# SSM products as two diagonal blocks, with the tables kept without their zero blocks

## The chip, the cores and the metric

The kernel runs on one core of one Trainium2 chip. The metric is the time of one execution on the device, in microseconds; a lower time is better. The times before are the median, the lowest and the highest of three runs. One further execution was profiled, and all rows of a profile in this document come from such an execution. The engines are named as in the profile: PE (TensorE matmuls), PEld (its weight loads), DVE (VectorE), ACT (ScalarE), POOL (GpSimd) and SP (SyncE, which here only issues DMAs). A name with a q (SPq, ACTq) is the engine's instruction queue, where DMA issues show.

## The reference, cut to what matters

One layer of a decoder: a SwiGLU block, a mixer with a state-space part (SSM) and windowed attention side by side, and a second SwiGLU block, for 256 prompt positions and 8 sequences of 4 sample positions. The SSM part is the one that the change touches. It has 64 groups of 16 channels with 64 complex states each:

```python
def s5_mixer(u, h0, A_re, A_im, B_re, B_im, C_re, C_im, D, log_dt, w_glu):
    lam_bar = jnp.exp(lam * dt)
    B_bar = ((lam_bar - 1.0) / lam)[..., None] * Bc
    bu = jnp.einsum('blgc,gpc->blgp', u32.astype(jnp.complex64), B_bar)
    bu = bu.at[:, 0].add(lam_bar * h0)
    a = jnp.broadcast_to(lam_bar, bu.shape)
    _, h = lax.associative_scan(_ssm_combine, (a, bu), axis=1)
    y = jnp.einsum('blgp,gcp->blgc', h, Cc).real + D.astype(f32) * u32
    y = jax.nn.gelu(y)
    y = y * jax.nn.sigmoid(jnp.einsum('blgc,gcd->blgd', y, w_glu.astype(f32)))
    return y, h[:, -1]
```

No group's input ever meets another group's states, so a product over two groups at once has two diagonal blocks and zeros elsewhere.

## The kernel before

**Columns.** All 288 positions lie in the free dimension: 4 phases of 72 columns (T = 4, W1 = 72: 8 sample columns and 64 prompt chunks). The SSM works on chunks of four positions. The 64 groups form 8 tiles (j = 0 to 7) of 4 pairs (q), two groups (g) to a pair; 128 partitions hold either 2 groups x 64 states, or 4 phases x 2 groups x 16 channels = 128 inputs of a pair.

**Slots.** The work is laid out by the weights (class `Weights`). They come in pieces of up to 128 x 1024; each piece is a slot. `W.next()` opens slot i: ACT casts piece i+2 into `wh` (L89), DVE subtracts to get the rest `wl` (L90), SP issues the load of piece i+5 (L81), then the extra work queued for slot i is issued, and then PE runs the piece: 24 matmuls of 288 columns for 1024, 18 for 768 and 15 for 640 (L273 to L275). `raw` has 5 buffers, `wh` and `wl` have 3. Within an engine the order is that of the program.

The first SwiGLU block takes slots 0 to 303: gate/up pieces (1024) in 0-51, a down phase in 52-83 (768, "12-wide"), gate/up to 131, down in 132-163 (12-wide), gate/up to 203, down in 204-235 (640, "10-wide"), gate/up to 271, and the last down phase in 272-303. The mix stage begins with slot 304.

**The tables (`precompute`).** From slot 24 on, one step per slot (`W.spread(24, precompute(qp))`, a step ends at a `yield`) computes each tile's SSM tables beside the first SwiGLU block. `common` has 31 steps, then `tile_tables(j)` 24 for each tile, counted from 0. Steps 14 and 15 of a tile turn the input tables (`bed`, L566) on PE and evict them (L568), step 16 makes the impulse response (L572), steps 17 to 20 copy it into place (L579 to L589), and step 22 writes the whole `stage` of the tile, six blocks of 128 x 512, to `mats[j]` in DRAM by one ACT DMA (L593). The blocks are: input table re and im (0, 1), impulse block (2), output table re and im (3, 4), rotation (5). In blocks 0 to 4 half of the entries are zeros, where one group of a pair would meet the other; `stage` and `bed` are cleared once (L446) and only the other halves are written.

**The mix stage.** For each tile j, with s = 304 + 2j + 5, extra work is queued for slots: `ssm_u_store` (ACT DMA of the projected input to `ud`, s), `ssm_load_a` (SP, blocks 0 and 1, s), `ssm_u_load` (SP, four DMAs that bring `ud` back in the order of phases, s+2), `ssm_load_r` (SP, s+2), `ssm_state` (PE L733, from s+5 on, then DVE and POOL for the scan), `ssm_load_b` (SP, blocks 2 to 4, s+6), `ssm_out` (PE L773 to L775, s+9), `ssm_y_store` (ACT, four DMAs, s+10), `ssm_y_load` (SP, `yn` and `gl`, s+11), `ssm_glu` (s+13). Tiles follow each other two slots apart, so that one period of two slots holds a state product, an output product, four U loads and four y stores, each of another tile.

**DMA semaphores.** The program gives the DMAs of SP and ACT eight completion semaphores in turn; a DMA that takes a semaphore waits for the one that had it eight DMAs before, whichever queue that was on.

Of the kernel before, what the change touches and what calls it, by code (L numbers as in the profile page):

```python
# [17 lines left out]
P = 128  # L18
# [99 lines left out]
def tile_hymba_step(ctx, tc, io):  # L118
# [226 lines left out]
    mats = [dr.tile([P, 5 * 512 + 512], F32, name="mats%d" % j) for j in range(8)]  # L345
# [5 lines left out]
    def precompute(qp):  # L351
# [10 lines left out]
        cst = small("cst", (P, 16 + 2 + NCH + 5))  # L362
        are, aim, ldt, dco = (prm[:, 32 * i:min(32 * i + 32, 104)] for i in range(4))
        eye, mgi, nrow, n5 = cst[:, 0:16], cst[:, 16:18], cst[:, 18:18 + NCH], cst[:, 18 + NCH:]
# [7 lines left out]
        stage = small("stage", (P, 6, 4, P))  # L372
        bed = [small("bed%d" % i, (P, 4, 4, 2, 16)) for i in range(2)]
        rep = [small("rep%d" % i, (P, 4, 2, 16)) for i in range(2)]
        small("gap_p", (P, 24))
# [62 lines left out]
        def common():  # L438
# [6 lines left out]
            for t_ in [stage] + bed + rep:  # L445
                pool_e.memset(t_, 0.0)  # L446
# [72 lines left out]
        def halves(ap):  # L519

            return [ap[64 * g:64 * g + 64].rearrange("p q (j g d) -> p q j g d", j=4, g=2)[:, :, :, g, :]
                    for g in range(2)]

        def tile_tables(j):
# [35 lines left out]
            rot = stage[:, 5].rearrange("p q (s k) -> p q s k", s=2)  # L560
            yield from cos_sin(rot[:, :, 0, :], rot[:, :, 1, :], f, t)
            yield
            for i in range(2):
                ps = pa.tile([P, 512], F32, name="main")
                for q_ in range(4):
                    pe.transpose(ps[:, q_ * P:(q_ + 1) * P],  # L566
                                 bed[i][:, q_].rearrange("p j g c -> p (j g c)"), ident)
                act.copy(stage[:, i].rearrange("p q m -> p (q m)"), ps)  # L568
# [24 lines left out]
            act.dma_start(mats[j], stage.rearrange("p a q m -> p (a q m)"))  # L593
# [38 lines left out]
def mix(tc, nc, io, es, W, base, e):  # L632
# [71 lines left out]
    def ssm_u_load(j):  # L704
        U[j] = sm.tile([P, 4, W1], F32, name="U", bufs=4)
        src = ud[j].rearrange("(q c) (j t) -> j c q t", q=4, j=T)
        for jr in range(T):
            get(U[j][32 * jr:32 * jr + 32], src[jr])
# [14 lines left out]
    def ssm_load_b(j):  # L723
        MB[j] = sm.tile([P, 3, 4, P], F32, name="mb", bufs=2)
        get(MB[j].rearrange("p a q m -> p (a q m)"), e["mats"][j][:, 1024:2560])
# [545 lines left out]
```

## Time and profile before

| | |
|---|---|
| median of 3 runs (lowest, highest) | 1998.82 us (1998.45, 1999.53) |
| the profiled execution | 1999.87 us, of which its span is 1998.1 |
| granted TensorE clock | 1.00 throughout |
| issue of `U<-ud` (SP) | 32 DMAs of 36 KB |
| issue of `yd<-yg` (ACT) | 32 DMAs of 36 KB |
| issue of `mats<-stage` (ACT) | 8 DMAs of 1536 KB |

Engines by stage, from the profile's windows (the columns are the stretch in us, its length, busy time of PE, PEld, DVE, ACT and POOL with the number of instructions, the granted clock, the share of the DMA engines and GB/s):

```profile
205.00:720.00 515.00, 515.00 (x3915) 514.15 (x3915) 328.46 (x553) 224.27 (x361) 47.10 (x81) 1.00 0.58 189
...
865.00:1000.00 135.00, 132.52 (x1039) 130.59 (x1039) 105.79 (x210) 49.26 (x90) 32.44 (x71) 1.00 0.77 251
```

The first stretch holds the tables of the eight tiles, the second the SSM part of the mix stage. A row of the chain or of a timeline begins with its start and its length in us, both from the span's start; a bracket at its end is the idle time ahead of it and what ended that. "xN" is the number of records merged in a row.

### The profile page before, as it was taken

To read this page: it belongs to the slowest core of one execution; us is meant where nothing else is said; L and a number is where in the kernel's file an instruction comes from. 1 tells how busy PE (TensorE), PEld (TensorE's weight loads), DVE (VectorE), ACT (ScalarE), POOL (GpSimd) and SP (SyncE) were. 2 spreads that over 40 slices of the span, in tenths; PEclk is the share of its full clock that TensorE was granted. 3 is DMA by queue.
4 is the path that set the end of the run, shared out by engine and by line. 5 is a ranking of instruction groups with operands and counts; after the bars stand their busy time and mean duration, and the time that the engine had idled before them with its cause. 6 is when DMAs were issued, how large, how long until landed. Compare 5 with 4: busy or idle time off the path is not lost.

```text
span 1998.1 us, 37634 instructions
## 1 busy us (share of the span) xinstructions
PE 1980.5 (99%) x15256; PEld 1968.0 (98%) x15256; DVE 1219.0 (61%) x1874; ACT 852.0 (43%) x1334; POOL 296.0 (15%) x450
## 2 busy tenths in 40 slices
PE   8999999999999999999999999999999999999999
PEld 7999999999999999999989999999999999999999
DVE  5577666566666654677888874555555455555554
ACT  5443444443444443543476553333333333333333
POOL 3110011000100000211368640000000000000000
PEclk9999999999999999999999999999999999999999
DMA  7555655546555664678744445555555555555555
GB/s 237 188 169 152 198 168 201 193 151 209 198 180 155 215 201 142 216 248 265 247 132 132 154 159 169 169 155 172 181 169 162 160 186 169 157 157 193 169 154 158
DMA packets 122622, 359.04 MB, mean 180 GB/s; under 512 B 22448, under 2 KB 30256, under 8 KB 121264
## 3 DMA queue, kind: packets, MB, share of 16 engines
q1 hardware_dynamic: 114672, 340.81, 53.5%
q10 hardware_dynamic: 7776, 15.83, 2.3%
q8 instruction: 119, 1.95, 0.4%
q14 instruction: 55, 0.45, 0.1%
HBM read 338.40 MB, written 20.22 MB: 179 GB/s over the span
## 4 chain that ended last, share of the span: by engine, by line
PE 96%; DMA 1%; POOL 1%; DVE 0%; SPq 0%; ACT 0%; issue 0%; POOLq 0%; ACTq 0%; DVEq 0%
PE main L273 31%; PE main L275 31%; PE main L274 31%; POOL acc L191 1%; PE main L733 1%; DMA yd<-yg 0%; PE main L566 0%; PE main L572 0%; DMA x<-in_x 0%; PE main L988 0%; DMA raw<-in_w_gu 0%; PE main L775 0%; PE main L774 0%; PE main L956 0%; PE main L773 0%; PE main L975 0%
## 5 line engine op out<-in xcount | busy, mean ns | idle before, releaser
L90 DVE TENSOR_TENSOR wl<-raw,wh 128x1024 fp32r<-128x1024 f32 (+2 forms) x680 | 758.6, 1116 | 526.2 <-ACT wh L89 521.1
L273 PE MATMUL main<-xh,wh 128*128 128x288 f32 x3136 | 924.4, 295 | 6.7 <-ACT xh L181 6.4
L275 PE MATMUL main<-xh,wl 128*128 128x288 f32 x3136 | 919.0, 293 | 2.2 <-DVE wl L90 2.2
L274 PE MATMUL main<-xl,wh 128*128 128x288 f32 x3136 | 918.4, 293 | 0.6 <-DVE xl L182 0.6
L89 ACT CAST wh<-raw 128x1024 fp32r<-128x1024 f32 (+2 forms) x680 | 643.1, 947 | 600.2 <-PE main L274 385.4
L273 PEld LDWEIGHTS main<-xh,wh 128*128 128x128 f32 x3136 | 589.5, 188 | 8.0 <-ACT xh L181 6.4
L275 PEld LDWEIGHTS main<-xh,wl 128*128 128x128 f32 x3136 | 589.3, 188 | 3.0 <-DVE wl L90 2.9
L274 PEld LDWEIGHTS main<-xl,wh 128*128 128x128 f32 x3136 | 589.5, 188 | 1.4 <-DVE xl L182 1.0
L273 PE MATMUL main<-hh,wh 128*128 128x288 f32 x1664 | 489.8, 294 | 0.0
L274 PE MATMUL main<-hl,wh 128*128 128x288 f32 x1664 | 487.9, 293 | 0.3 <-DVE hl L684 0.3
L275 PE MATMUL main<-hh,wl 128*128 128x288 f32 x1664 | 487.8, 293 | 0.0
L274 PEld LDWEIGHTS main<-hl,wh 128*128 128x128 f32 x1664 | 312.6, 188 | 0.7 <-DVE hl L684 0.5
L273 PEld LDWEIGHTS main<-hh,wh 128*128 128x128 f32 x1664 | 312.5, 188 | 0.5 <-DVE t L1095 0.2
L275 PEld LDWEIGHTS main<-hh,wl 128*128 128x128 f32 x1664 | 312.5, 188 | 0.0
L300 POOL TENSOR_TENSOR s<-s,R 128x288 f32<-128x288 f32 x88 | 71.3, 810 | 1228.0 <-ACT s L299 1228.0
L299 ACT ACTIVATE s<-t 128x288 f32<-128x288 f32 x88 | 39.2, 445 | 233.5 <-DVE t L298 233.5
L309 ACT CAST hh<-h 128x288 fp32r<-128x288 f32 x88 | 38.2, 434 | 235.5 <-DVE h L308 235.5
L330 DVE SCALAR_TENSOR_TENSOR x<-main,x 128x288 f32<-128x288 f32 x128 | 58.4, 456 | 52.3 <-PE main L275 51.1
L308 DVE TENSOR_TENSOR h<-main,s 128x288 f32<-128x288 f32 x88 | 40.2, 457 | 70.3 <-PE main L275 69.9
L298 DVE TENSOR_TENSOR t<-main,R 128x288 f32<-128x288 f32 x88 | 40.2, 457 | 59.4 <-PE main L275 59.2
L310 DVE TENSOR_TENSOR hl<-h,hh 128x288 fp32r<-128x288 f32 x88 | 40.3, 458 | 44.0 <-ACT hh L309 44.0
L191 POOL TENSOR_TENSOR acc<-acc,sq 128x288 f32<-128x288 f32 x45 | 48.4, 1075 | 45.8 <-ACT sq L187 44.4
(266 smaller groups left out, 891.0 us busy)
## 6 DMA issues: line engine op xcount, KB each, us to landing
raw<-in_w_gu SPq DMA_DIRECT2D x352, 512.0 KB, 3.5
raw<-in_w_dn SPq DMA_DIRECT2D x128, 384.0 KB, 3.0
raw<-in_w_dn SPq DMA_DIRECT2D x128, 320.0 KB, 3.0
raw<-in_w_in SPq DMA_DIRECT2D x40, 512.0 KB, 4.7
raw<-in_w_out SPq DMA_DIRECT2D x32, 512.0 KB, 3.4
mats<-stage ACTq DMA_DIRECT2D x8, 1536.0 KB, 7.1
mb<-mats SPq DMA_DIRECT2D x8, 768.0 KB, 5.3
ma<-mats SPq DMA_DIRECT2D x8, 512.0 KB, 4.2
```

The costliest lines, as they stand in the source:

```text
L89: self.nc.scalar.copy(wh[:, :n], t[:, :n])
L90: self.nc.vector.tensor_tensor(wl[:, :n], t[:, :n], wh[:, :n].bitcast(F32), op=ALU.subtract)
L191: eng.tensor_tensor(acc, acc, sq, op=ALU.add)
L273: pe.matmul(ps, wh[:, s], rh[k], start=first and a == 0, stop=False)
L274: pe.matmul(ps, wh[:, s], rl[k], start=False, stop=False)
L275: pe.matmul(ps, wl[:, s], rh[k], start=False, stop=last and a == n - 1)
L298: dve.tensor_tensor(t1, pg[:, :N], R, op=ALU.mult)
L299: act.activation(s1, t1, AF.Silu)
L300: pool_e.tensor_tensor(s2, s1, R, op=ALU.mult)
L308: dve.tensor_tensor(h, pu[:, :N], s2, op=ALU.mult)
L310: dve.tensor_tensor(hl, h, hh.bitcast(F32), op=ALU.subtract)
L330: dve.scalar_tensor_tensor(x[d], ps[:, :N], 0.5, x[d], op0=ALU.mult, op1=ALU.add)
```

## The change

The two groups of a pair get partitions 0-63 and 64-127 in every operand, so that the order of a pair's 128 inputs becomes group, phase, channel in place of phase, group, channel.

- `mats[j]` shrinks from 128 x 3072 to 128 x 1792: the zero halves of the blocks are not kept, so that each input and output table is 128 x 256, as is the impulse block.
- `ssm_state` and `ssm_out` make two products of 64 x 64 x 72 where one of 128 x 128 x 72 stood, one for each half of the partitions, both into the same PSUM tile (one bank).
- `ssm_u_load` and `ssm_y_store` use eight DMAs of 16 partitions per tile in place of four of 32.
- In the tables, `bed` has no room for the other group (two DVE operations in place of four), the turned table is 64 partitions high and is evicted in four copies of 64 partitions in place of two of 128, and the output tables are copied by two POOL copies in place of four.
- The impulse block is no longer put together by 16 copies on ACT and DVE: after three DMAs (input tables, rotation, output tables, one step) 32 ACT DMAs of 16 partitions x 64 write it into `mats[j]`, eight in each of four steps. `kk` is kept for all tiles with three blocks of zeros behind its four, from which the DMAs read the upper part of the block. The masks `mgi` and the product with them (`km`) go.
- A tile's tables have 26 steps in place of 24: the three DMAs are step 19, the 32 are steps 20 to 23.

```diff
-    mats = [dr.tile([P, 5 * 512 + 512], F32, name="mats%d" % j) for j in range(8)]
+    mats = [dr.tile([P, 1024 + 768], F32, name="mats%d" % j) for j in range(8)]
...
-        stage = small("stage", (P, 6, 4, P))
-        bed = [small("bed%d" % i, (P, 4, 4, 2, 16)) for i in range(2)]
+        st_a = small("st_a", (P, 2, 4, 64))
+        st_r = small("st_r", (P, 4, P))
+        st_c = small("st_c", (P, 2, 4, 64))
+        kk = small("kk", (P, 7, 16))
+        bed = [small("bed%d" % i, (P, 4, 4, 16)) for i in range(2)]
...
-            for t_ in [stage] + bed + rep:
+            for t_ in [kk] + rep:
                 pool_e.memset(t_, 0.0)
...
@@ -529,9 +527,8 @@
             t = qp.tile(bx, F32, name="xt")
             yield from cmul(xr, xi, bc[:, 2, q, None, :].to_broadcast(bx), bc[:, 3, q, None, :].to_broadcast(bx),
                             erd[:, q, :, None].to_broadcast(bx), eid[:, q, :, None].to_broadcast(bx), t, True)
-            for i, src in ((3, xr), (4, xi)):
-                for g, dst in enumerate(halves(stage[:, i])):
-                    pool_e.tensor_copy(dst, src[64 * g:64 * g + 64, :, 0:4, :])
+            for i, src in enumerate((xr, xi)):
+                pool_e.tensor_copy(st_c[:, i].rearrange("p q (j d) -> p q j d", j=4), src[:, :, 0:4, :])
                 yield
             bx = [P, 4, 4, 16]
             br = bb[:, 0, q, None, :].to_broadcast(bx)
@@ -545,52 +542,54 @@
             tt(tc_, br, pi, op=ALU.mult)
             tt(td, bi, pr, op=ALU.mult)
             yield
+            tt(bed[0], ta, tb, op=ALU.subtract)
+            tt(bed[1], tc_, td, op=ALU.add)
+            yield
             for g in range(2):
                 pp = slice(64 * g, 64 * g + 64)
-                tt(bed[0][pp, :, :, g, :], ta[pp], tb[pp], op=ALU.subtract)
-                tt(bed[1][pp, :, :, g, :], tc_[pp], td[pp], op=ALU.add)
                 for i in range(2):
                     pool_e.tensor_copy(rep[i][pp, :, g, :], bb[pp, i, q])
-                yield
+            yield
             bx = [P, 4, NCH]
             f = qp.tile(bx, F32, name="rf")
             t = qp.tile(bx, F32, name="rtm")
             yield from frac(f, t, psh[:, q, None].to_broadcast(bx), psl[:, q, None].to_broadcast(bx),
                             nrow[:, None, :].to_broadcast(bx))
-            rot = stage[:, 5].rearrange("p q (s k) -> p q s k", s=2)
+            rot = st_r.rearrange("p q (s k) -> p q s k", s=2)
             yield from cos_sin(rot[:, :, 0, :], rot[:, :, 1, :], f, t)
             yield
             for i in range(2):
                 ps = pa.tile([P, 512], F32, name="main")
                 for q_ in range(4):
-                    pe.transpose(ps[:, q_ * P:(q_ + 1) * P],
-                                 bed[i][:, q_].rearrange("p j g c -> p (j g c)"), ident)
-                act.copy(stage[:, i].rearrange("p q m -> p (q m)"), ps)
+                    pe.transpose(ps[:64, q_ * P:(q_ + 1) * P],
+                                 bed[i][:, q_].rearrange("p j c -> p (j c)"), ident)
+                v = ps[:64].rearrange("p (q g m) -> p q g m", q=4, g=2)
+                for g in range(2):
+                    act.copy(st_a[64 * g:64 * g + 64, i], v[:, :, g, :])
                 yield
             ps = pa.tile([P, 512], F32, name="main")
             for i, xx in ((0, xr), (1, xi)):
                 pe.matmul(ps[:, :256], rep[i].rearrange("p q g c -> p (q g c)"), xx[:, :, 1:5, :],
                           start=i == 0, stop=i == 1)
             yield
-            kk = qp.tile([P, 4, 16], F32, name="kk")
-            km = qp.tile([P, 4, 2, 16], F32, name="km")
             for q_ in range(4):
                 pp = slice(32 * q_, 32 * q_ + 32)
-                act.copy(kk[pp].rearrange("p n d -> p (n d)"), ps[pp, 64 * q_:64 * q_ + 64])
+                act.copy(kk[pp, 0:4].rearrange("p n d -> p (n d)"), ps[pp, 64 * q_:64 * q_ + 64])
             yield
             tt(kk[:, 3], kk[:, 3], de[:, j], op=ALU.add)
-            for gi in range(2):
-                ts(km[:, :, gi, :], kk, mgi[:, gi:gi + 1], None, op0=ALU.mult)
+            yield
+            m = mats[j]
+            act.dma_start(m[:, 0:512], st_a.rearrange("p a q m -> p (a q m)"))
+            act.dma_start(m[:, 512:1024], st_r.rearrange("p q m -> p (q m)"))
+            act.dma_start(m[:, 1280:], st_c.rearrange("p a q m -> p (a q m)"))
             yield
             for jr in range(4):
+                tk = kk[:, 3 - jr:7 - jr].rearrange("p n d -> p (n d)")
                 for q_ in range(4):
-                    (act.copy, cp_)[q_ % 2](
-                        stage[32 * jr:32 * jr + 32, 2, q_, :32 * jr + 32],
-                        km[32 * q_:32 * q_ + 32, 3 - jr:].rearrange("p n g d -> p (n g d)"))
-                if jr % 2:
-                    yield
-            yield
-            act.dma_start(mats[j], stage.rearrange("p a q m -> p (a q m)"))
+                    for g in range(2):
+                        r, o = 64 * g + 16 * jr, 1024 + 64 * q_
+                        act.dma_start(m[r:r + 16, o:o + 64], tk[32 * q_ + 16 * g:32 * q_ + 16 * g + 16])
+                yield
             yield
             yield
 
@@ -703,17 +702,19 @@
 
     def ssm_u_load(j):
         U[j] = sm.tile([P, 4, W1], F32, name="U", bufs=4)
-        src = ud[j].rearrange("(q c) (j t) -> j c q t", q=4, j=T)
+        src = ud[j].rearrange("(q g c) (j t) -> j g c q t", q=4, g=2, j=T)
         for jr in range(T):
-            get(U[j][32 * jr:32 * jr + 32], src[jr])
+            for g in range(2):
+                r = 64 * g + 16 * jr
+                get(U[j][r:r + 16], src[jr, g])
 
     def ssm_load_a(j):
-        MA[j] = sa.tile([P, 2, 4, P], F32, name="ma", bufs=2)
-        get(MA[j].rearrange("p a q m -> p (a q m)"), e["mats"][j][:, :1024])
+        MA[j] = sa.tile([P, 2, 4, 64], F32, name="ma", bufs=2)
+        get(MA[j].rearrange("p a q m -> p (a q m)"), e["mats"][j][:, :512])
 
     def ssm_load_r(j):
         ROT[j] = sa.tile([P, 4, 2, NCH], F32, name="rot", bufs=2)
-        get(ROT[j].rearrange("p q s k -> p (q s k)"), e["mats"][j][:, 2560:])
+        get(ROT[j].rearrange("p q s k -> p (q s k)"), e["mats"][j][:, 512:1024])
 
     def ssm_decay(j):
         D0[j] = sa.tile(c4, F32, name="d0", bufs=2)
@@ -721,8 +722,8 @@
         pool_e.memset(D0[j][:, :, 0:1], 0.0)
 
     def ssm_load_b(j):
-        MB[j] = sm.tile([P, 3, 4, P], F32, name="mb", bufs=2)
-        get(MB[j].rearrange("p a q m -> p (a q m)"), e["mats"][j][:, 1024:2560])
+        MB[j] = sm.tile([P, 3, 4, 64], F32, name="mb", bufs=2)
+        get(MB[j].rearrange("p a q m -> p (a q m)"), e["mats"][j][:, 1024:])
 
     def ssm_state(j):
         ma, u, rot = MA.pop(j), U[j], ROT.pop(j)
@@ -730,7 +731,8 @@
         for i in range(2):
             ps = aux()
             for q in range(4):
-                pe.matmul(ps[:, q * W1:(q + 1) * W1], ma[:, i, q], u[:, q], start=True, stop=True)
+                for pp in (slice(0, 64), slice(64, 128)):
+                    pe.matmul(ps[pp, q * W1:(q + 1) * W1], ma[pp, i, q], u[pp, q], start=True, stop=True)
             b.append(ps[:, :N].rearrange("p (q t) -> p q t", q=4))
         br, bi = b[0][:, :, NB:], b[1][:, :, NB:]
         co, si = rot[:, :, 0, :], rot[:, :, 1, :]
@@ -769,18 +771,19 @@
         mb, u, cs = MB.pop(j), U.pop(j), CS.pop(j)
         ps = aux()
         for q in range(4):
-            o = ps[:, q * W1:(q + 1) * W1]
-            pe.matmul(o, mb[:, 0, q], u[:, q], start=True, stop=False)
-            pe.matmul(o, mb[:, 1, q], cs[:, 0, q, :W1], start=False, stop=False)
-            pe.matmul(o, mb[:, 2, q], cs[:, 1, q, :W1], start=False, stop=True)
+            for i, rhs in enumerate((u[:, q], cs[:, 0, q, :W1], cs[:, 1, q, :W1])):
+                for pp in (slice(0, 64), slice(64, 128)):
+                    pe.matmul(ps[pp, q * W1:(q + 1) * W1], mb[pp, i, q], rhs[pp], start=i == 0, stop=i == 2)
         YG[j] = sm.tile([P, 4, W1], F32, name="yg", bufs=1)
         act.activation(YG[j].rearrange("p q t -> p (q t)"), ps[:, :N], AF.Gelu_apprx_tanh)
 
     def ssm_y_store(j):
         yg = YG.pop(j)
-        dst = yd[j].rearrange("(q c) (j t) -> j c q t", q=4, j=T)
+        dst = yd[j].rearrange("(q g c) (j t) -> j g c q t", q=4, g=2, j=T)
         for jr in range(T):
-            put(dst[jr], yg[32 * jr:32 * jr + 32])
+            for g in range(2):
+                r = 64 * g + 16 * jr
+                put(dst[jr, g], yg[r:r + 16])
 
     def ssm_y_load(j):
         YN[j] = sm.tile([P, N], F32, name="yn", bufs=2)
```

More of the change, by code (lines that the diff above doesn't have):

```diff
@@ L361, in precompute @@
         bc = small("bc", (P, 4, 32, 16))
-        cst = small("cst", (P, 16 + 2 + NCH + 5))
+        cst = small("cst", (P, 16 + NCH + 5))
         are, aim, ldt, dco = (prm[:, 32 * i:min(32 * i + 32, 104)] for i in range(4))
-        eye, mgi, nrow, n5 = cst[:, 0:16], cst[:, 16:18], cst[:, 18:18 + NCH], cst[:, 18 + NCH:]
+        eye, nrow, n5 = cst[:, 0:16], cst[:, 16:16 + NCH], cst[:, 16 + NCH:]
         sh = small("tmps", (P, 8, 32))
@@ L371, in precompute @@
         de = small("de", (P, 8, 16))
-        stage = small("stage", (P, 6, 4, P))
-        bed = [small("bed%d" % i, (P, 4, 4, 2, 16)) for i in range(2)]
+        st_a = small("st_a", (P, 2, 4, 64))
[3 more added lines that the diff above has]
+        bed = [small("bed%d" % i, (P, 4, 4, 16)) for i in range(2)]
         rep = [small("rep%d" % i, (P, 4, 2, 16)) for i in range(2)]
-        small("gap_p", (P, 24))
+        small("gap_p", (P, 40))
         def vexp(src, em1=None, ex=None):
@@ L517, in common @@
                 yield from tile_tables(j)
-        def halves(ap):
-            return [ap[64 * g:64 * g + 64].rearrange("p q (j g d) -> p q j g d", j=4, g=2)[:, :, :, g, :]
-                    for g in range(2)]
         def tile_tables(j):
@@ L1137, in constants @@
     f = np.float32
-    cst = np.zeros((P, 16 + 2 + NCH + 5), f)
+    cst = np.zeros((P, 16 + NCH + 5), f)
     r = np.arange(P)
     cst[r, r % 16] = 1
-    cst[r, 16 + (r // 16) % 2] = 1
-    cst[:, 18:18 + NCH] = T * (1 + np.arange(NCH))
-    cst[:, 18 + NCH:] = np.arange(5)
+    cst[:, 16:16 + NCH] = T * (1 + np.arange(NCH))
+    cst[:, 16 + NCH:] = np.arange(5)
     j, k = r // 32, r % 32
```

## The prediction

> **What bounds the kernel now.** I read the page's head and its chain of work first, then the chain in order of time where the changed products run, then PE's timeline there.
>
> ```profile
> span 1998.1 us, 37634 instructions
> PE 1980.5 (99%) x15256; PEld 1968.0 (98%) x15256; DVE 1219.0 (61%) x1874; ACT 852.0 (43%) x1334; POOL 296.0 (15%) x450
> ...
> PE 96%; DMA 1%; POOL 1%; DVE 0%; SPq 0%; ACT 0%; issue 0%; POOLq 0%; ACTq 0%; DVEq 0%
> ```
>
> PE carries 96% of the chain: a microsecond taken from it is won and one added is lost, unless something else is late at that place. The chain prices the products (start, length, line):
>
> ```profile
> 887.88 1.74 PE main L733 x16
> ...
> 909.22 0.17 PE main L773 x2
> ...
> 911.85 0.18 PE main L273
> ```
>
> A state product takes 1.74 us for 16 records (8 products; each f32 product shows two records). An output product takes 911.85 - 909.22 = 2.63 us for 24. That is 0.11 per record, and 0.18 for the projection matmul behind. There are eight of each. PE waits beside them only twice, both times for a DMA:
>
> ```profile
> 927.08 1.98 PE L733 MATMUL main<-U,ma 128*128 128x72 f32 x16 [1.24 <-DMA U<-ud]
> ...
> 933.52 0.72 PE L794 MATMUL main<-yn,gl 128*128 128x288 f32 x2 [1.24 <-DMA gl<-in_w_glu]
> ```
>
> **Term A: the products on PE.** Each product becomes two, on partitions 0-63 and 64-127, so the records double to 32 and 48. The question is whether the two blocks run beside each other. The nearest rows:
>
> ```profile
> 223.62 0.86 PE main L572 x4
> ...
> 991.50 0.87 PE main L956 x12
> 992.37 0.33 PE main L273
> ...
> 1064.43 1.04 PE main L1059 x32
> ```
> ```profile
> L572 PE MATMUL main<-xr,rep 128*128 128x256 f32 x16 | 4.7, 378 | 0.0
> ...
> L1059 PE MATMUL main<-pc,cv 128*64 128x16 f32 x64 | 2.2, 210 | 0.0
> ```
>
> L572 moves 256 columns in 0.86 / 4 = 0.215 us per record, so 72 columns take 0.061. L1059 alternates two column halves of 64 and moves only 16 columns: 32 records in 1.04, which is 17 steps of 0.061 if the halves overlap with one step of stagger. That step is then the load of 64 columns. So a record of one block takes 0.061 either way. Side by side, a state product is 17 steps, 1.04, and an output product 25 steps, 1.53. I add 0.12 for filling an emptied array (an estimate: L956 has 12 records of 128 columns on two row halves, and 0.12 of its 0.87 is left beyond 7 steps of 0.215 / 2) and take 0.33 for the matmul behind, as L273 shows after L956. State: 1.04 + 0.12 + 0.33 = 1.49 against 1.92, -0.43. Output: 1.98 against 2.81, -0.83. Eight of each: **-10.1**. One after the other, 32 and 48 steps give 2.40 and 3.38: +0.48 and +0.57 each, **+8.4**. I take the first, since L1059's halves, in one bank, overlap.
>
> Here a rule speaks against the change. The Trainium skill, "TensorEngine Tiling (Array Packing)", section Restrictions and Gotchas, says that different row tiles cannot access the same PSUM bank at the same time. Before's row-split products write two banks, so no run here shows it; by that sentence the sum takes +8.4 for -10.1.
>
> The transposes (eight per tile) now load 64 columns but still move 128:
>
> ```profile
> 217.97 0.44 PE main L566 x4
> ...
> 1091.29 0.22 PE main L1044 x2
> 1091.51 0.14 PE main L273
> ```
>
> L566 takes 0.11 each and so does L1044, which loads only 32 columns; the matmul behind it takes 0.14. So I put them at nothing. The same page of the Trainium skill, section Tiling Modes, says that a change of the tiling mode drains the array. The 0.33 above agrees, the 0.14 doesn't. By the rule 16 groups of transposes would add 16 x (0.33 - 0.14) = 3.0.
>
> **Term B: 35 DMAs per tile on ACT in place of one.** In the last steps of a tile's tables ACT issues three DMAs in one slot, then eight in each of four slots. Queued behind them are the casts to `wh`, without which PE stops.
>
> ```profile
> 238.78 0.83 ACT L89 CAST wh<-raw 128x768 fp32r<-128x768 f32 x1 [1.53 <-PE main L274]
> 238.86 0.35 ACTq L593 DMA_DIRECT2D mats<-stage  x1
> 241.18 0.84 ACT L89 CAST wh<-raw 128x768 fp32r<-128x768 f32 x1 [1.56 <-PE main L274]
> ...
> 651.64 0.73 ACT L89 CAST wh<-raw 128x640 fp32r<-128x640 f32 x1 [1.22 <-PE main L274]
> 651.72 0.33 ACTq L593 DMA_DIRECT2D mats<-stage  x1
> 653.63 0.73 ACT L89 CAST wh<-raw 128x640 fp32r<-128x640 f32 x1 [1.27 <-PE main L274]
> ...
> 915.03 1.05 ACT L89 CAST wh<-raw 128x1024 fp32r<-128x1024 f32 x1 [2.73 <-PE main L274]
> 915.05 1.98 ACTq L783 DMA_DIRECT2D yd<-yg  x4
> 917.13 0.41 ACT L720 COPY d<-e 128x256 f32<-128x256 f32 x1 [1.05 <-issue]
> ...
> 940.08 1.76 ACTq L783 DMA_DIRECT2D yd<-yg  x4
> ```
>
> The distance of two casts is the slot: 2.40 us in the 12-wide down phases (18 matmuls), 2.00 in the 10-wide ones, so 3.20 for the 24 matmuls of gate and up. Four y stores in a row hold ACT for 1.76 to 1.98, and the copy behind starts when they are out; a lone DMA takes 0.33 to 0.35. I take 0.47 for each of eight in a row and 0.1 per slot, 3.86 us of ACT. The excess over the slot is 1.46, 1.86 or 0.66, and after four slots the cast is 5.8, 7.4 or 2.6 late. What hides it is a lead of two slots: the cast in slot i is for slot i+2, and DVE's subtraction must follow it:
>
> ```profile
> L90 DVE TENSOR_TENSOR wl<-raw,wh 128x768 fp32r<-128x768 f32 x128 | 122.8, 959 | 90.9 <-ACT wh L89 90.4
> L90 DVE TENSOR_TENSOR wl<-raw,wh 128x640 fp32r<-128x640 f32 x128 | 106.5, 832 | 75.8 <-ACT wh L89 75.1
> ```
>
> 12-wide: 4.80 - 0.83 - 0.96 = 3.0 of cover, so a burst stalls PE by 2.8. 10-wide: 4.00 - 0.73 - 0.83 = 2.4, a stall of 5.0. Gate and up: 6.40 - 1.05 - 1.28 (0.96 x 1024 / 768) = 4.1 against 2.6, no stall.
>
> Which tile falls where follows from the steps. The tables start in slot 24; 31 steps come before the first tile; a tile had 24 and gets 26; the small DMAs are steps 20 to 23. So tile j's burst starts in slot 75 + 26j: 75, 101, 127, 153, 179, 205, 231, 257. Slots 52-83 and 132-163 are 12-wide down phases, 204-235 a 10-wide one. Tiles 0 and 3 fall in the first kind, 5 and 6 in the second, the others in gate and up. Before's rows bear the count out: its tile 0 stores at step 22, slot 77, eight slots behind its transposes (slot 69, 217.97), and 238.86 is that many 12-wide slots later. Term B: 2 x 2.8 + 2 x 5.0 = **+15.6**. Ends: at 0.33 per issue only the 10-wide bursts lose 0.6 each, +1.2. At 0.525 (917.13 - 915.03 for four) the stalls are 4.2 and 6.4, +21.
>
> The edits of copies and memsets on ACT, DVE and POOL lie in the idle time between casts (the brackets above) and bring and cost nothing; without that cover they would be worth under 2 us per tile. The 16 more slots end the tables in slot 263 of 304, still ahead of their first load.
>
> **Term C: the loads of the mix stage.** A tile's tables shrink from 1536 to 896 KB, but U's loads and y's stores go from 4 + 4 DMAs to 8 + 8. SP's waits, a period of the chain, SP's timeline in it, mb's issues (KB, us to landing), and the landing times of U and then of y:
>
> ```profile
> SPq L789 <- DMA yd<-yg: 5.7, 2, 4.5
> ```
> ```profile
> 940.12 1.74 PE main L733 x16
> ...
> 951.47 1.74 PE main L733 x16
> ```
> ```profile
> 942.96 0.33 SPq L789 DMA_DIRECT2D gl<-in_w_glu  x1
> ...
> 943.87 0.38 SPq L725 DMA_DIRECT2D mb<-mats  x1
> 944.29 1.90 SPq L708 DMA_DIRECT2D U<-ud  x4
> ```
> ```profile
> mb<-mats SPq DMA_DIRECT2D x8, 768.0 KB, 5.3
> ```
> ```profile
> DMA to landing us min/median/max: 1.8/4.8/9.2
> ```
> ```profile
> DMA to landing us min/median/max: 1.7/3.8/6.5
> ```
>
> `gl` loads an input, yet waits for a y store. The two share only a completion semaphore: eight go round over the DMAs of SP and ACT, and each DMA waits for the one eight before it. So in this stage SP follows ACT's stores: first store at 940.08, U's issues from 944.29 (4.2 later) for 1.9, landed 4.8 after that, 951.0. The state product that needs U starts at 951.47. PE's period is 11.35, the DMA chain's 10.9. Afterwards PE wants 11.35 - 0.43 - 0.83 = 10.1, and the chain has eight U issues: 4.2 + 3.8 + 4.8 = 12.8. Behind the U loads on SP stand rot, ma and the weights, five pieces ahead, so only U itself is late. In the five periods whose U loads run among ud stores, y stores and tables (states 3 to 7) PE then waits 12.8 - 10.1 = 2.7: **+13.5**. Ends: with U landing in 1.8 the chain is 9.8, the term 0, and the two waits of 1.24 go, -2.5. If mb waits for a store 1.4 later, as eight stores make it, and the last U for mb's landing (5.3 at its old size), the chain is 4.2 + 1.4 + 5.3 + 0.4 + 4.8 = 16.1: +30. In the bursts of term B these semaphores add no wait, since eight issues take 3.8 and a short store lands in 1.7.
>
> **The sum** is made against the profiled execution, 1999.87 us (1998.1 and 1.8 around it), 1.05 above the median of 1998.82. -10.1 + 15.6 + 13.5 = +19.0; 1998.8 + 19 = **2018**.
>
> **The rivals.** (1) The DMA chain keeps up, since each tile moves 640 KB less: 1998.8 - 10.1 + 15.6 = 2004. Against it: the chain had only 0.45 us to spare. (2) Faster: a DMA of 16 partitions is cheap, issued in 0.33 and landed in 1.8. Then the bursts hide in the casts' lead, the chain (4.2 + 2.6 + 1.8) stays under PE's 10.1, and the gain stands: 1998.8 - 10.1 + 1.2 = 1990. It decides from 0.39 per issue down, where term B is 5.5. Against it: four stores of 32 partitions in a row took no less than 0.44. (3) The change doesn't do what it says, since the blocks of a product run one after the other: +8.4; PE wants 12.4 per period and waits 0.4 in five: 1998.8 + 8.4 + 15.6 + 2 = 2025. The Trainium skill's sentence on one bank, above, is the case for it.
>
> **Chances.** Forecast 0.52, (1) 0.20, (2) 0.15, (3) 0.13. A measurement of this kernel can tell about 0.2%, 4 us, from no change. Faster is (2) and a sliver of (1), 0.16; within 0.2% is the low part of (1), with the 2.5 back, 0.08; slower is the rest, 0.76. 8 in 10 lie in 1994 to 2038: this takes in (1), (3) and the long ends of B and C, and leaves out (2).
>
> **What would show it.** A: L733 at 1.2 us for 32 records and the output product at 1.65 in the chain; 2.1 and 3.0 if the blocks follow each other. B: casts that fall behind by 1.5 to 1.9 per slot, and PE waiting for `wh` or `wl` in four places, near 240, 465, 625 and 680 us, and not in gate and up; eight issues in 3.7 us, or in 2.6 for (2). C: PE waits for `U` before states 3 to 7, and these start 12 to 13 us apart; 10 if C is wrong. A time near 1990 would make both B and C wrong.

## The result: 3% slower, and the profile after

The changed kernel takes **2058.52 us** (median of 4, 2055.94 to 2062.12), the kernel before took 1998.63 beside it: ratio 1.0301, 95% interval 1.0288 to 1.0314. The forecast was 2018, with a range to 2038: the sign was right, the loss three times as large as forecast.

The profiled execution took 2062.12 us, 62.2 above that of before (1999.87). From its page: the head, then the shares of the chain by engine and by line.

```profile
span 2060.3 us, 38479 instructions
PE 2008.8 (97%) x15576; PEld 1979.8 (96%) x15576; DVE 1189.6 (58%) x1778; ACT 836.0 (41%) x1286; POOL 284.3 (14%) x432
...
PE 83%; DMA 8%; DVE 3%; ACTq 2%; ACT 2%; issue 1%; POOL 1%; SPq 0%; POOLq 0%; DVEq 0%
PE main L273 27%; PE main L275 27%; PE main L274 27%; DMA mats<-kk 2%; DMA raw<-in_w_gu 2%; ACTq L591 2%; DVE wl L90 2%; DMA yd<-yg 1%; ACT wh L89 1%; DMA raw<-in_w_dn 1%; POOL acc L191 1%; DMA ud<-t 1%; PE main L776 1%; DMA gl<-in_w_glu 0%; DMA mats<-st_a 0%
```

PE carried 96% of the chain and carries 83%. What came in its place is a mixture: small DMAs (`kk`), their issues on ACT, weight loads, casts. No single wait of that size exists.

Three marks in PE's timeline show where the time went: the first state product, the last one, and line 338's product early in the second feed-forward.

| us | before | after | difference |
|---|---|---|---|
| first state product starts | 887.71 | 933.65 | +45.9 |
| first to last state product | 75.4 | 90.1 | +14.7 |
| last state product to line 338 | 238.1 | 239.7 | +1.6 |
| line 338 to the end of the span | 796.9 | 796.8 | -0.1 |

So 46 us are lost while the tables are built, 16 in the mix stage, none after it.

The products did what term A said. In the chain of work in order of time (start, length, line) an output product and a state product of the changed kernel:

```profile
961.37 1.65 PE main L776 x48
...
1023.83 1.15 PE main L735 x32
```

48 records in 1.65 us and 32 in 1.15, where the forecast had 1.53 + 0.12 and 1.04 + 0.12. The two blocks run beside each other, and both write one bank. The sentence of the Trainium skill, "TensorEngine Tiling (Array Packing)", Restrictions and Gotchas, that different row tiles cannot access one PSUM bank at the same time would have made them 3.0 and 2.1, as the forecast worked out: for diagonal blocks of 64 x 64 these rows say otherwise.

In the bursts, ACT's timeline during tile 1 (gate and up), with DMA issues as ACTq; the bracket is the wait ahead of an instruction and what ended it:

```profile
315.39 1.05 ACT L89 CAST wh<-raw 128x1024 fp32r<-128x1024 f32 x1 [1.16 <-PE main L274]
315.42 6.05 ACTq L591 DMA_DIRECT2D mats<-kk  x8
321.57 0.44 ACT L299 ACTIVATE s<-t 128x288 f32<-128x288 f32 x1 [5.12 <-DMA mats<-kk]
...
322.02 3.26 ACTq L591 DMA_DIRECT2D mats<-kk  x7
325.38 1.05 ACT L89 CAST wh<-raw 128x1024 fp32r<-128x1024 f32 x1 [2.43 <-DMA mats<-kk]
325.41 5.11 ACTq L591 DMA_DIRECT2D mats<-kk  x8
```

Seven issues in a row took 3.26, which is the 0.47 each of the forecast. But the bursts of eight at 315.42 and 325.41 took 6.05 and 5.11. The chain of work in order of time at the same place shows what they stood for:

```profile
315.52 4.54 DMA raw<-in_w_gu
...
320.07 0.31 ACTq L591
...
321.67 1.31 DMA mats<-kk
...
322.99 1.24 DVE wl L90
...
324.24 3.44 DMA raw<-in_w_gu
...
327.71 0.36 ACTq L591
```

A small DMA of `kk` is issued when a weight load has landed, though they share no data; later the next weight load is on the chain behind the casts that stood behind small DMAs. This is the round of eight completion semaphores that the forecast used in term C. In term B it was denied.

In the mix stage, PE's waits of the changed kernel (in total, times, longest), SP's timeline, and PE's timeline at one of these waits:

```profile
PE main L797 <- DMA gl<-in_w_glu: 7.7, 3, 5.0
PE main L735 <- DMA U<-ud: 7.5, 3, 4.2
```
```profile
943.36 9.58 SPq L709 DMA_DIRECT2D U<-ud  x8
...
955.38 7.47 SPq L709 DMA_DIRECT2D U<-ud  x8
```
```profile
954.35 2.64 PE L735 MATMUL main<-U,ma 64*64 64x72 f32 x32 [4.20 <-DMA U<-ud]
...
957.32 0.44 PE L274 MATMUL main<-xl,wh 128*128 128x288 f32 x1
957.56 0.44 PE L275 MATMUL main<-xh,wl 128*128 128x288 f32 x1
...
959.21 0.30 PE L273 MATMUL main<-xh,wh 128*128 128x288 f32 x1
959.35 0.30 PE L274 MATMUL main<-xl,wh 128*128 128x288 f32 x1
```

The two groups of eight U issues shown take 9.6 and 7.5 us, and over the eight tiles they take 4.7 to 9.6, not 3.8, and PE waits. Half of the wait is not for `U` but for `gl`, an input (7.7 us against 7.5). The chain ahead of its longest wait:

```profile
991.91 5.89 DMA yd<-yg
...
997.87 0.32 SPq L790
...
998.24 2.73 DMA gl<-in_w_glu
...
1001.11 1.30 PE main L797 x2
```

`gl` stands on SP behind the load of `yn` (L790), and that behind a y store which took 5.89 us to land.

The timeline at 954.35 shows something the forecast did not have at all: behind the 4.20 us wait the state product takes 2.64, and the matmuls start 0.24 us apart in place of 0.13, for about 4.8 us. The windows give the cause in the column PEclk, the granted clock (third from the end; full speed is 1.00):

```profile
950.00:956.00 6.00, 1.78 (x24) 1.48 (x24) 4.76 (x8) 1.79 (x4) 2.13 (x5) 0.70 0.54 152
956.00:961.00 5.00, 5.00 (x39) 4.86 (x36) 1.51 (x4) 0.00 (x0) 0.00 (x0) 0.68 0.83 277
...
933.00:1024.00 91.00, 75.82 (x820) 70.00 (x820) 58.63 (x125) 25.57 (x48) 15.83 (x41) 0.89 0.64 194
```

Between the first and the last state product the clock is at 0.89 of full speed; the mean of before's whole span is 1.00. The Trainium skill, "TensorE: Matmul & The Clock Gate", Part 1, says that the array's clock is halved after an idle window of some 3.4 us and comes back after a busy one. The trace agrees that the clock halves around a wait and comes back (4.20 idle, 4.8 at half speed behind it), but not that it takes so long an idle time: a wait of 1.89 us was enough, with PE busy for 1.11 of the 3 us around it.

```profile
1015.98 0.72 PE L797 MATMUL main<-yn,gl 128*128 128x288 f32 x2 [1.89 <-DMA gl<-in_w_glu]
```
```profile
1014.00:1017.00 3.00, 1.11 (x14) 0.67 (x15) 1.80 (x5) 1.85 (x5) 1.88 (x5) 1.00 0.87 212
1017.00:1021.00 4.00, 4.00 (x50) 3.57 (x47) 1.39 (x2) 1.31 (x4) 0.00 (x0) 0.57 0.58 177
```

Two questions were left. What makes up the 46 us, when ACT's time was forecast to cost 15.6? And why do the matmuls of the table stage stand 0.1333 us apart nearly everywhere in the changed kernel, where before had long stretches at 0.1300? The windows show the second one: the same 85 us without a gap, before and after.

```profile
720.00:805.00 85.00, 85.00 (x656) 85.00 (x655) 43.26 (x53) 33.36 (x44) 5.59 (x7) 1.00 0.51 158
```
```profile
825.00:910.00 85.00, 85.00 (x640) 85.00 (x639) 52.56 (x77) 43.10 (x73) 17.04 (x17) 1.00 0.64 197
```

656 matmuls for 640 at the same granted clock. In the table stage the spacing changes only where PE does a tile's table work (lines 564 and 572) or waits; it then stays for hundreds of matmuls. Before is at 0.1300 behind five of its eight tiles.

### The profile page after: what moved, and what is told of

It is laid out like the page before. It is cut to its first block, busy times and chain, and to the rows that moved or that the text cites. A ratio compares the mean times of both kernels' runs of the same rounds, so it can differ in the third digit from the quotient of the medians.

```text
span 2060.3 us, 38479 instructions
## 1 busy us (share of the span) xinstructions
PE 2008.8 (97%) x15576; PEld 1979.8 (96%) x15576; DVE 1189.6 (58%) x1778; ACT 836.0 (41%) x1286; POOL 284.3 (14%) x432
## 4 chain that ended last, share of the span: by engine, by line
PE 83%; DMA 8%; DVE 3%; ACTq 2%; ACT 2%; issue 1%; POOL 1%; SPq 0%; POOLq 0%; DVEq 0%
PE main L273 27%; PE main L275 27%; PE main L274 27%; DMA mats<-kk 2%; DMA raw<-in_w_gu 2%; ACTq L591 2%; DVE wl L90 2%; DMA yd<-yg 1%; ACT wh L89 1%; DMA raw<-in_w_dn 1%; POOL acc L191 1%; DMA ud<-t 1%; PE main L776 1%; DMA gl<-in_w_glu 0%; DMA mats<-st_a 0%
## 5 line engine op out<-in xcount | busy, mean ns | idle before, releaser
L273 PEld LDWEIGHTS main<-xh,wh 128*128 128x128 f32 x3136 | 592.8, 189 | 14.7 <-ACT xh L181 6.5
L275 PE MATMUL main<-hh,wl 128*128 128x288 f32 x1664 | 493.2, 296 | 4.3 <-DVE wl L90 4.0
L300 POOL TENSOR_TENSOR s<-s,R 128x288 f32<-128x288 f32 x88 | 71.3, 810 | 1254.0 <-ACT s L299 1238.2
L330 DVE SCALAR_TENSOR_TENSOR x<-main,x 128x288 f32<-128x288 f32 x128 | 58.4, 457 | 57.3 <-PE main L275 55.6
```

Of the source, the lines that this page charges most:

```text
L273: pe.matmul(ps, wh[:, s], rh[k], start=first and a == 0, stop=False)
L275: pe.matmul(ps, wl[:, s], rh[k], start=False, stop=last and a == n - 1)
L300: pool_e.tensor_tensor(s2, s1, R, op=ALU.mult)
L330: dve.scalar_tensor_tensor(x[d], ps[:, :N], 0.5, x[d], op0=ALU.mult, op1=ALU.add)
```

## The experiments

All stand against the kernel before, run beside them. Every edit is to the changed kernel, unless it says otherwise. Theory 1 was the shared semaphores, theory 2 ACT's issue time alone.

**The burst away.**

```diff
+            act.dma_start(m[:, 1024:1280], xr.rearrange("p q n d -> p (q n d)")[:, 0:256])
             for jr in range(4):
...
-                        act.dma_start(m[r:r + 16, o:o + 64], tk[32 * q_ + 16 * g:32 * q_ + 16 * g + 16])
                 yield
```

> The 32 small DMAs of a tile are left out; one DMA of 128 x 256 numbers that are at hand stands in their place, so the impulse block's values are not the reference's. All else is the changed kernel. Every theory in which the bursts cost what the table stage lost (45.7 us, the end of the first feed-forward at 910.4 for 864.6) brings that end back to 865 and the time to 2058.5 - 45.7 = 2013. The rival: the matmuls of the table stage stand 0.1334 us apart in place of 0.1300 for another reason than the bursts (the transposes of 64 columns, other addresses); then about 12 of the 45.7 us stay, and the time is 2025.

Measured: 2020.55 us, ratio 1.0103 (1.0088 to 1.0118). The first state product starts at 897.20. So the bursts cost 36.4 us by the first state (933.65 - 897.20), but 9.5 of the 45.9 stay (897.20 - 887.71), and the spacing stays at 0.1333. The rival was right on that part.

**ACT's time without the DMAs**, in two lengths.

```diff
             for jr in range(4):
+                for _ in range(8):
+                    act.copy(xs, xr)
                 yield
```

This is e2_fill, on top of e1_one (`xs` is the buffer `xt`, free by then); e5_fill192 copies `[:, :, 0:3, :]` of both.

> As e1_one, but with ACT's queue filled: in each of the four slots eight copies of 128 x 320 on ACT, about 0.45 us each, stand where the eight small DMAs were. ACT is held as long as my prediction had it, and no DMA is added. Theory 1, the eight shared completion semaphores (each DMA waits for the one eight before it, so raw loads wait for small stores and ACT for raw loads): ACT's time alone costs what the prediction said or less, 1 to 16 us over e1_one, 2014 to 2029. Theory 2, ACT's time alone makes the whole loss: about 2058 again.

> As e2_fill, but each of the eight copies is 128 x 192, about 0.39 us, so that ACT with its cast takes 0.73 + 3.1 = 3.85 us per slot: the length that the prediction gave a burst (the impulse block's values are not the reference's, as in e1_one). Theory 1, the prediction's formula (excess over the slot, less the casts' lead) holds and the changed kernel's bursts are longer than 3.86: e1_one + 15.6 = 2036, with about 2.8 us more in tiles 0 and 3, 5.0 in tiles 5 and 6, none in 1, 2, 4 and 7. Theory 2, the lead is smaller than the formula says: every tile loses, 2045 to 2060.

Measured: e2_fill 2060.72, ratio 1.0299 (1.0283 to 1.0316); e5_fill192 2034.31, ratio 1.0161 (1.0135 to 1.0188). The first looks like a win for theory 2, until its ACT timeline is read:

```profile
233.81 3.90 ACT L589 COPY xt<-xr 128x320 f32<-128x320 f32 x8
237.62 0.83 ACT L89 CAST wh<-raw 128x768 fp32r<-128x768 f32 x1
238.35 3.90 ACT L589 COPY xt<-xr 128x320 f32<-128x320 f32 x8
```

A cast and eight copies take 238.35 - 233.81 = 4.54 us per slot, for the forecast's 3.86. A DMA's issue runs beside the cast that stands ahead of it (315.39 and 315.42 above); a copy doesn't. e2_fill was a burst 18% longer than forecast, and by chance as long as the changed kernel's own turn out to be (below). e5_fill192 has the forecast's length and costs 13.8 more than e1_one, for the forecast's 15.6; its place is right too. Here is the time from one tile's impulse product on PE (line 572) to the next, less the same time in e1_one, whose eight are 74.5, 84.9, 71.3, 72.9, 84.9, 57.3, 74.1 and 155.5 us (the last to the first state product):

| us lost in tile | 0 | 1 | 2 | 3 | 4 | 5 | 6 | 7 | sum |
|---|---|---|---|---|---|---|---|---|---|
| forecast, 3.86 per slot | 2.8 | 0 | 0 | 2.8 | 0 | 5.0 | 5.0 | 0 | 15.6 |
| e5_fill192 | 2.1 | 0 | 0 | 2.1 | 0 | 4.0 | 4.5 | 0 | 12.7 |
| forecast's formula with after's own bursts | 4.5 | 1.9 | 0.8 | 4.7 | 2.4 | 5.9 | 9.5 | 2.9 | 32.5 |
| after | 4.9 | 2.1 | 1.5 | 4.7 | 2.9 | 7.5 | 9.0 | 3.2 | 36.0 |
| e2_fill | 7.0 | 2.8 | 4.4 | 5.5 | 2.8 | 9.0 | 6.0 | 2.8 | 40.1 |

The third line takes each tile's four bursts as ACT's timeline shows them (tile 1: 6.05 + 3.57 + 5.11 + 3.65 = 18.4, and 0.1 per slot; 18.8 - 4 x 3.20 - 4.1 = 1.9). The sums are of unrounded figures. The 32 bursts hold ACT for 143 us, 4.5 each, in place of 3.76: a tile's first and third burst take 3.8 to 6.4, its second and fourth 3.5 to 4.6. So the formula and the lead were right to within 1.6 us in each tile; the bursts were longer than forecast, by what ACT stood waiting for earlier DMAs. Of the 143 - 120 = 23 us, 17 come through (32.5 - 15.6).

**The same DMAs from SP, and from POOL** (`act.dma_start` becomes `sp.dma_start` or `pool_e.dma_start`).

> The 32 small DMAs of a tile are issued by SP, in the same four steps. Same semaphores, but ACT's casts no longer stand behind them. Theory 1: the loop ACT DMA - raw load - cast - ACT DMA is open; SP still waits for each DMA's predecessor, about 4.3 us per eight (the landing of a raw load), 4.8 per slot of nine, against slots of 2.0 to 3.2, so SP falls behind by 6 to 11 us in a burst, against five pieces (10 to 16 us) of lead: nothing to 3 us per burst, 2013 to 2035. Theory 2: ACT is free, 2013. Theory 3, small packets themselves slow the weights' loads: no change, 2058.

> The 32 small DMAs of a tile are issued by POOL, which has completion semaphores of its own and little work in this stage. Theory 1 and 2: the loss of the table stage goes, 2013, unless POOL's issue is slow enough to hold the table steps of POOL. Theory 3, small packets themselves slow the weights' loads: stays near 2058.

Measured: e3_sp 2022.54, ratio 1.0112 (1.0092 to 1.0132); e4_pool 2023.40, ratio 1.0113 (1.0096 to 1.0130). First state products at 898.40 and 897.38, as in e1_one. The 256 small DMAs themselves cost next to nothing (2 to 3 us over e1_one, and the intervals overlap), so theory 3 falls. SP's timeline of e3_sp in tile 1:

```profile
306.64 5.35 SPq L591 DMA_DIRECT2D mats<-kk  x8
312.63 0.35 SPq L81 DMA_DIRECT2D raw<-in_w_gu  x1
313.02 3.66 SPq L591 DMA_DIRECT2D mats<-kk  x8
```

The first eight still take 5.35, but no cast stands behind them, and SP has five pieces of lead. What costs is that ACT's queue holds both the casts and DMAs that wait for other DMAs.

Those others are not only the weight loads. POOL's DMAs complete on eight semaphores of their own in the trace (111 to 118; SP's and ACT's on eight others from 100 to 108), and still its 32 bursts take 134.5 us for 122 at its 0.48 per issue. POOL's timeline of e4_pool in tile 0:

```profile
230.10 5.48 POOL L591 DMA_DIRECT2D mats<-kk  x11 [37.11 <-DVE kk L579]
237.54 5.72 POOL L591 DMA_DIRECT2D mats<-kk  x12 [1.97 <-DMA mats<-kk]
244.25 4.29 POOL L591 DMA_DIRECT2D mats<-kk  x9 [0.99 <-DMA mats<-kk]
```

So some 12 us of waiting come from the small stores alone, each for the one eight before it; ACT had 23. How those 23 divide between weight loads and small stores no run shows.

**The transposes.** As e4_pool, with `bed` of 128 columns, half of them zeros.

> As e4_pool (small DMAs issued by POOL), and the transposes get 128 columns again, 64 of them zeros that nothing reads. In the table stage the matmuls stand 0.1333 us apart behind every tile's PE work, where before had 0.1300 behind five of eight. Theory S1, the transposes of 64 columns set that: five stretches are back at 0.1300, the first state starts near 888, the time is 2023 - 10 = 2013. Theory S2, something else sets it (where the tables lie in SBUF, the step at which they fall): no change, 2023.

Measured: 2021.29, ratio 1.0106 (1.0088 to 1.0123); the first state at 898.29, the spacing still 0.1333. S1 falls; the width of the transposes costs nothing, as forecast.

**Term C alone**, on the kernel before:

```diff
         for jr in range(T):
-            get(U[j][32 * jr:32 * jr + 32], src[jr])
+            for g in range(2):
+                r = 32 * jr + 16 * g
+                get(U[j][r:r + 16], src[jr, 16 * g:16 * g + 16])
...
-            put(dst[jr], yg[32 * jr:32 * jr + 32])
+            for g in range(2):
+                r = 32 * jr + 16 * g
+                put(dst[jr, 16 * g:16 * g + 16], yg[r:r + 16])
```

> The kernel before, with only U's loads and y's stores cut to 8 + 8 pieces of 16 partitions: term C alone. The prediction's chain through the shared semaphores: states 12.8 us apart where they were 10.8, over five to seven periods +10 to +14, 2009 to 2013, PE waits for U. The rival, the pieces are hidden or land so much faster: 1999. In the first case PE's gain on the products cannot show in the changed kernel, because PE is not what sets the period.

Measured: 2024.99, ratio 1.0125 (1.0106 to 1.0145). States 14.3 us apart (100.3 / 7), and from the first state to line 338 340.4 us for before's 313.5: **+26.9**, twice the forecast. The windows of e8_pieces from its first to its last state:

```profile
886.00:986.00 100.00, 87.91 (x576) 85.66 (x576) 58.55 (x126) 25.59 (x47) 15.73 (x41) 0.85 0.66 216
```

PE is idle for 12.1 of the 100 us, where before had its two waits of 1.24, and the clock is at 0.85. The waits that the chain of DMAs makes (9.6 more) are of the size that was forecast; the clock's 100 x 0.15 = 15 us come on top.

**One DMA in place of eight.** With the rows of a block in the order group, channel, step, the rows of U lie in `ud` at one even distance, so U's load and y's store are one DMA each, and a tile's round trip through DRAM has 4 DMAs for the changed kernel's 18 and before's 10. (The tables are permuted to match.)

```diff
-        for jr in range(T):
-            for g in range(2):
...
+        get(U[j], ud[j].rearrange("(q r) (j t) -> (r j) q t", q=4, j=T))
...
+        put(yd[j].rearrange("(q r) (j t) -> (r j) q t", q=4, j=T), yg)
...
+            for jr in range(4):
+                pool_e.tensor_copy(kw[:, jr], kk[:, :, 3 - jr:7 - jr])
...
+            for q_ in range(4):
+                dst = m[:, 1024 + 64 * q_:1088 + 64 * q_].rearrange("(r j) n -> r j n", j=4)
+                act.dma_start(dst, kw[32 * q_:32 * q_ + 32].rearrange("p j d n -> p j (d n)"))
+                yield
```

> The changed kernel, with the rows of a block in the order group, channel, step in place of group, step, channel. U's load and y's store are then one DMA each (10 DMAs of a tile's round trip become 4), and the impulse block is spread on chip into four windows and written by 4 DMAs of 32 partitions, one per slot. The products stay as changed. If bursts and pieces are the whole loss beside the matmul spacing: the table stage as in e1_one (first state near 897), the mix at PE's rate, before's 313.5 us from the first state to the second feed-forward less 10.1 and less its two waits of 1.24, 301; with 10 us of wider spacing left the time is about 1999 + 10 - 12.6 = 1996. If the products do not bring their 10 us: 2007. If the spacing goes as well: 1986.

Measured: 1998.79, ratio 0.9996 (0.9986 to 1.0005), level with before. First state to line 338: 301.8 us, for 301 expected. PE's waits in that stretch name no DMA any more; the longest are

```profile
PE main L273 <- DVE t L1091: 1.0, 1, 1.0
PE main L942 <- ACT qsq L929: 0.8, 2, 0.6
```

So the products do bring their time, once the transfers around them don't take it back. And the first state is still late, at 898.24: what is left is the spacing.

**What sets the spacing.** The change makes the tables ahead of `rep` smaller by 4096 - 2160 = 1936 words (`stage` and two `bed` of 3072 + 1024 go, `st_a`, `st_r`, `st_c`, `kk` and two `bed` of 512 + 512 + 512 + 112 + 512 come), which is 60.5 x 128 bytes of a partition. (`cst`, further ahead, also loses two words; no run shows whether that moves `rep`.) `gap_p` grew by the missing 64 bytes, but it stands behind `rep`.

```diff
+        small("gap_k", (P, 16))
         rep = [small("rep%d" % i, (P, 4, 2, 16)) for i in range(2)]
-        small("gap_p", (P, 40))
+        small("gap_p", (P, 24))
```

e10_gap is e9_order with this, e11_24 is e9_order with its four DMAs in two slots, e12_both has both edits.

> e9_order with 16 words of padding moved from behind the repeated input matrices to ahead of them, so that they begin at the same place within 128 bytes as in the kernel before (the other tables as in e9_order). The question is what sets the wider matmul spacing in the table stage (0.1333 for 0.1300 us behind five of the eight tiles' PE work, 10 us by the first state). If it is the place of the operand of that PE work, the first state comes 10 us earlier, near 888, and the time is 1989. If not, 1999.

> e9_order with 24 steps per tile in place of 26 (its four DMAs of the impulse block in two slots), so that every tile's PE work falls in the slot where the kernel before has it. If the slot sets the wider spacing, the stretches behind tiles 1, 2, 4, 5 and 7 go back to 0.1300, and the time is 1989. If not, 1999.

> Both edits of e10_gap and e11_24. If the place and the slot are needed together, 1989 here and 1999 in the two others. If all three stay near 1999, neither sets the spacing.

Measured: e10_gap **1988.61**, ratio 0.9950 (0.9933 to 0.9966); e11_24 1999.32, 1.0000 (0.9991 to 1.0009); e12_both **1987.48**, 0.9944 (0.9929 to 0.9959). First states at 886.64, 899.41 and 886.49. It is the place of `rep`, which alone moves between e9_order and e10_gap, by 64 bytes, and not the slot. The same window in e9_order and in e10_gap:

```profile
750.00:835.00 85.00, 85.00 (x640) 85.00 (x639) 45.00 (x61) 36.32 (x54) 9.99 (x14) 1.00 0.53 173
```
```profile
750.00:835.00 85.00, 85.00 (x656) 85.00 (x656) 47.65 (x67) 38.97 (x61) 12.28 (x13) 1.00 0.57 178
```

e10_gap is at 0.1300 behind the same five tiles as before. e10_gap and e12_both are also faster than both kernels, half a per cent below before.

**The same 64 bytes in the changed kernel itself.**

> The changed kernel itself, with e10_gap's edit alone: 16 words of padding moved from behind the repeated input matrices to ahead of them. The account so far of the changed kernel's loss against before is: bursts 36, U and y pieces 26, products -10, place 10, sum 62. With the place as in before 10 of them go: 2058.5 - 10 = 2048. If the place matters only where PE doesn't wait, it is less, 2050 to 2055; if the stalls of the bursts hide it wholly, 2058.

Measured: 2058.33, ratio 1.0289 (1.0275 to 1.0303). Nothing is won: in PE's timeline five stretches start at 0.1300 again, but each falls back to 0.1333 once its tile's burst has made PE wait. So the two costs don't add: with the place mended the bursts cost 46.5 us by the first state (933.15 - 886.64 of e10_gap), without it 36.4.

## Why the prediction was wrong: bursts, pieces, and two costs that were not in the sum

| term, us | forecast | measured | from |
|---|---|---|---|
| A, products | -10.1 | -11.7 | 301.8 (e9_order) - 313.5; the two waits of 1.24 that went with U's and y's four pieces are in it, -9.2 without |
| B, bursts | +15.6 | +36.4 | 933.65 - 897.20 (e1_one) |
| C, pieces | +13.5 | +28.0 | 329.8 - 301.8 (e9_order); +26.9 in e8_pieces |
| place of `rep` | not seen | +9.5 | 897.20 - 887.71 |
| sum | +19.0 | +62.2 | 2062.12 - 1999.87 |

The measured rows are steps along one line, so they add up by construction; e13_gap shows that the rows of the bursts and of `rep` overlap, so that another order of steps would share them out otherwise.

- **Term A** was right in mechanism and size, and so was the choice of trace over rule: the two blocks run side by side.
- **Term B** failed in one sentence: "In the bursts of term B these semaphores add no wait, since eight issues take 3.8 and a short store lands in 1.7". The 1.7 is the least landing of y's stores in a view whose median is 3.8; `kk`'s stores land in 2.4 in the median and in up to 4.8. And eight DMAs in a row are one full round of the semaphores, so among them are successors of the weight loads (landing 3.6 us in the median), of the three table stores (3.3 to 4.8) and of other small stores. A burst takes 4.5 us, not 3.76, and gate and up's tiles, "no stall", lose 1.5 to 3.2 each. The formula with the lead of two slots held, and so did the places. The long end, +21 at 0.525 per issue, leaves out the 0.1 per slot; with it the stalls are 4.6, 6.8 and 0.3, +24, still short of +36.4.
- **Term C** had the right mechanism. The mean period came out as forecast, 12.8 for 90.1 / 7 = 12.9 measured, but partly by luck: single periods run from 8.4 to 18.0, and the half clock is in them. Three things were wrong.
  - The term was counted for five periods against PE's 10.1; with the products in place PE needs 65.2 / 7 = 9.3, and over all seven the difference is 7 x (12.9 - 9.3) = 24.9.
  - "So only U itself is late" failed: PE waited 7.7 us for `gl` and 7.5 for `U`, and for `U` before three states, not five.
  - The forecast took a wait as costing its own length. Between the first and the last state product PE was idle for 91.00 - 75.82 = 15.2 us, near the 13.5 forecast; the clock at 0.89 took another 91 x 0.11 = 10.0. Together, 25.2, they make up the 24.9 to within the rounding.

  Before's own trace had a sign that issues wait, too: its groups of four U issues took 1.75 to 7.11 us, not always 1.9.

```profile
904.83 7.11 SPq L708 DMA_DIRECT2D U<-ud  x4
```

- **The half clock** shows in the bursts too: windows of the changed kernel in tile 6's.

```profile
706.00:709.00 3.00, 1.45 (x10) 0.98 (x8) 0.82 (x1) 0.72 (x1) 0.00 (x0) 1.00 0.15 42
709.00:712.00 3.00, 2.72 (x14) 2.37 (x14) 0.15 (x1) 0.72 (x1) 0.00 (x0) 0.67 0.55 182
712.00:715.00 3.00, 2.99 (x11) 2.64 (x12) 1.05 (x2) 0.00 (x0) 0.00 (x0) 0.50 0.40 127
```

  The longest waits there are 1.23 and 0.32 us; PE was busy for half of 706 to 709, and the clock fell all the same. What that costs here is not shown: tile 6 lost 9.0 us where the formula, which knows no clock, gives 9.5, since PE has to wait for the late casts in any case. No run explains the 3.5 us by which after loses more in all than the formula gives (36.0 - 32.5).
- **The place of `rep`** was not in the sum. The diff of the kernels shows it: the padding tile `gap_p` is changed from 24 to 40 words, and it stands behind the tile that moves.
- **The rivals.** (1), that the DMA chain keeps up, and (2), that short DMAs are cheap, fell with e8_pieces and the SP timeline. (3), blocks one after the other, fell with the first chain rows. What came was the forecast's own mechanisms at twice their size, with the half clock, and the place of `rep`; no rival had any of it.
- **Open:** why 64 bytes in the operand of sixteen products set the spacing of thousands of other matmuls. That they do is shown by e10_gap against e9_order; no run shows how, nor why tiles 0, 3 and 6 stay at 0.1333 in both places.

## What to carry to other kernels

Where engines share a small ring of completion semaphores, count DMAs and not bytes: with as many in a row as the ring has places, a DMA can wait for a stranger or for its own forerunner, and a queue that also holds work on the critical path hands that wait on. Look for a row order that makes a permuting transfer one DMA before cutting it into pieces. Price a wait of PE with the half-speed matmuls behind it, and where a change resizes tiles in a kernel with padding tiles, work out what moves within 128 bytes.

## What the runs showed of the hardware that was not expected

- The same chain of matmuls of 128 x 128 by 288 columns has two lasting spacings at full granted clock, 0.1300 and 0.1333 us. It changes only at other PE work or a wait, and which one follows depends, behind five of the eight tiles, on where the operand of that work lies, by 64 bytes: 10 us of this kernel.
- Waits of 1.23 and 0.32 us close together, with PE busy about half of 3 us, and a single one of 1.89 halved the clock as one wait of 4.20 did.
- 256 DMAs of 4 KB cost 2 to 3 us in all, not clear of the noise, when issued by SP or POOL (e3_sp and e4_pool against e1_one) and 38 when issued by ACT.
